# First modulation tile in four loads, bias columns in their rows, x ahead of 256 weight columns, and more warming products, at the opening of a decoder layer

## The chip, the cores and the metric

The kernel runs on one core of one Trainium2 chip. The metric is the device time of one execution in microseconds: the median of 3 runs is 735.68 us (735.65 to 735.8). The engines are named as the profile has them: TensorE (PE, with its weight loads as PEld), VectorE (DVE), ScalarE (ACT), GpSimd (POOL) and SyncE (SP), which here only issues DMAs.

## The reference

One decoder layer: attention of two kinds on a modulated input, merged by gates, and a gated feed-forward part. The change concerns only the beginning, the modulation and the first projection:

```
mod = c @ w_ada + b_ada
sh1, sc1, gt1, sh2, sc2, gt2 = [m[:, None, :] for m in jnp.split(mod, N_MOD, axis=-1)]

u = x * (1.0 + sc1) + sh1
proj = u @ w_in
q_a, k_a, v_a, f_a, q_b, k_b, v_b, g_a, g_b = jnp.split(proj, _split_points(), axis=-1)
```

x has 512 rows of 1024 columns, w_ada is 1024 by 6144, w_in 1024 by 5128. All is in 32-bit floating point. Each of the six parts of mod has 1024 values, which the kernel holds as 8 tiles of 128.

## The kernel before

**Products in three.** Full precision is had by splitting each operand into a high part in a reduced format (ScalarE copies it: wh of a weight, uh of the modulated input) and the rest (VectorE subtracts: wl, ul). Each product is then three: high with high, low weight with high input, high weight with low input.

**Opening.** The first stage runs over 8 tiles of 128 input channels. For tile j it needs two modulation values for each channel (kind 0, the shift, and kind 1, the scale), each a sum over 1024 products of c with a row of w_ada. VectorE forms such a sum in one instruction over a row of w_ada and a copy of c that stands in every partition (`mod_sum`, L241), and adds the bias (`bcols`). Then ScalarE or VectorE forms uh and ul of the tile (`first_mod`), ScalarE and VectorE split the 904 weight columns of the tile (`first_split`, `first_pad`), and TensorE accumulates 23 products of 512 columns (`first_mm`, L361) into the banks `grp[0..7]`: three for each of the column groups 0 to 6, and two for the padded forget gate columns (`fpad`, group 7).

**Tile 0** has its own path, since nothing can run before it. c is broadcast by 8 small products (L235) into the banks 6 and 7, and the sums for tile 0 read c from there; ScalarE copies it into `cbc` afterwards (L337), which the sums of all other tiles read. The two modulation rows of tile 0 come in two loads: `wa[0]` holds the first half of both kinds, `wa[1]` the second half of both. So there are four sums of 512 columns, two for each load. Between the third and the fourth, VectorE adds the first halves to the biases (L287); the last addition (L289) gives `modc`. The weight columns of tile 0 come as 384 and 520 columns, with x between them (L258 to L260).

**Order of the work.** Each engine runs its instructions in the order written, partly rearranged by a scheduler, which places an instruction where its model of the time finds it ready; `tc.issue_after` ties an instruction behind another on this engine. SyncE issues loads in the order written. At most eight loads are outstanding: each later one waits until the eighth before it has landed. The loads of c (4 KB) and of the biases (`bcols`, 24 KB, 192 bytes for each partition) are issued by ScalarE (L103, L105).

**Warming.** While TensorE waits for tile 0 it multiplies zeros (`heat`, L230): 5 products before the broadcast, 3 after it, and then 1, 1 and 2 behind the second, third and fourth sum.

The order of the products of tile 0 is by `rank`: high with high of the groups 0 to 2, low weight of the same, then high with high of 3 and 4, and so on.

After the first stage (from 50 us) the second one begins with the weights of the attention heads; `split_proc` (L217 on ScalarE, L94 on VectorE) splits them.

Of the kernel before, what the change touches and what calls it, by code (L numbers as in the profile page):

```python
# [46 lines left out]
CUT = 5  # L47
FILL = (15, 18, 18), (11, 11, 11)
# [3 lines left out]
def layer_kernel(ctx: ExitStack, tc: tile.TileContext, out, xT, x, c8, wa0, wa1, bcol, w1, wct, wv, bf,  # L52
# [50 lines left out]
    S.dma_start(c8s, c8)  # L103
    bcols = const([P, 6, KT], F32, "bcols")
    bcd = S.dma_start(bcols, bcol)  # L105
# [24 lines left out]
    for q in (slice(1, 2), slice(3, 6)):  # L130
        S.activation(bcols[:, q, :], bcols[:, q, :], AF.Copy, bias=1.0)
# [97 lines left out]
    def heat(n):  # L229
        return [PE.matmul(grp[5], warm[:, 0:P], warm, start=True, stop=True) for _ in range(n)]  # L230
# [17 lines left out]

    x0 = early.tile([P, 512], F32, name="x0", tag="x0")

    def first_load(j):
        wa = [early.tile([P, D], F32, name=nm("wa"), tag="wa", bufs=5) for _ in range(2)]
        r = stg.tile([P, 1024], F32, name=nm("raw"), tag="raw", bufs=LOADS)
        xt = z(F32, "xt")
        if j == 0:
            for e in range(2):
                nc.sync.dma_start(wa[e], wa0[j, e])
            nc.sync.dma_start(r[:, 0:384], w1[j][:, 0:384])  # L258
            nc.sync.dma_start(x0, xT[j * P : (j + 1) * P, :])
            nc.sync.dma_start(r[:, 384:W1C], w1[j][:, 384:W1C])  # L260
        else:
            nc.sync.dma_start(wa[0], wa0[j, 0])
            if j == 1:
                nc.sync.dma_start(wa[1], wa0[j, 1])
            nc.sync.dma_start(r[:, 0:W1C], w1[j])
            if j > 1:
                nc.sync.dma_start(wa[1], wa0[j, 1])
            nc.sync.dma_start(xt, xT[j * P : (j + 1) * P, :])
            if j == 6:
                nc.sync.dma_start(bfs, bf)  # L270
        pend[j] = [wa, xt, r]

    def first_acc(j):
        wa = pend[j][0]
        if j == 0:
            s = state["chl"]
            for e in range(2):
                for q in range(2):
                    c = slice(q * 512, (q + 1) * 512)
                    with tc.issue_after(s.ins):  # L280
                        s = mod_sum(q, j, wa[e], c, e, grp[6 + e])
                    if e or q:
                        for m in heat(WARM[2] + e * q):
                            paced(m, s)
                    if e and not q:
                        with tc.issue_after(s.ins):
                            s = V.tensor_tensor(bcols[:, 0:2, j], bcols[:, 0:2, j], modr[:, 0:2, j, 0], ALU.add)  # L287
# [6 lines left out]
    def first_split(j):  # L294
# [3 lines left out]
        if j:  # L298
            hi_of(h[:, 0:W1C], r[:, 0:W1C])
        else:  # L300
            state["h"] = S.activation(h[:, 0:384], r[:, 0:384], AF.Copy)
        pend[j][2:] = [h, l, r]

    def first_pad(j):
        h, l, r = pend[j][2:]
        if j == 0:
            c = slice(384, W1C)
# [5 lines left out]
    def first_mod(j):  # L313
# [12 lines left out]
        else:  # L326
# [5 lines left out]
            c = slice(384, W1C)  # L332
# [5 lines left out]
            with tc.issue_after(ts.ins):  # L338
                ts = lo_of(l[:, 0:384], r[:, 0:384], h[:, 0:384])
# [15 lines left out]
    def first_mm(j, gs):  # L355
        ops = [(g, n, m) for g in gs for n, m in enumerate(first_ops(j, g))]
        if j < KT - 1:
            rank = (0, 2, 4, 1, 3, 5)
            ops.sort(key=(lambda o: rank[o[1]] + 3 * (o[0] > 2) if o[0] < 5 else o[1] + 3 * (o[0] == 7)) if j == 0 else lambda o: o[1] + 3 * (o[0] == 7))
# [976 lines left out]
def _pack(inputs):  # L1336
# [10 lines left out]
    wa0 = wt[0:2].transpose(1, 0, 2, 3).copy()  # L1347
    wa0[0] = wa0[0].reshape(2, P, 2, D // 2).transpose(2, 1, 0, 3).reshape(2, P, D)
    r["wa0"] = c(wa0)
    r["wa1"] = c(wt[2:6].reshape(32, P, D))  # L1350
    bm = a["b_ada"].reshape(6, KT, P)
    r["bcol"] = c(bm[[0, 1, 3, 4, 2, 5]].transpose(2, 0, 1))
# [29 lines left out]
_NAMES = ["xT", "x", "c8", "wa0", "wa1", "bcol", "w1", "wct", "wv", "bf", "wp", "wo", "lncol", "lnrow",  # L1382
# [20 lines left out]
```

## Time and profile before

| what | value |
|---|---|
| median of 3 runs | 735.68 us |
| the profiled execution, whole | 736.08 us |
| its span, first to last instruction | 734.3 us |
| mean granted TensorE clock | 0.997 |
| TensorE busy | 724.3 us, 99% |
| VectorE busy | 599.7 us, 82% |
| ScalarE busy | 390.1 us, 53% |
| first product of the layer | 8.00 us |
| TensorE busy from 8.00 to 50.40 us | 42.40 of 42.40 us |
| TensorE busy from 470 to 727 us | 256.49 of 257.00 us |
| TensorE busy from 727 us to the end | 0.00 of 7.30 us |

TensorE works almost without a pause from the first product of the layer to 727 us; before it lies the opening, behind it the last normalisation. How such a profile is read: a row of the timeline gives the start, the length, the engine, the line, what is written and read, and in brackets the idle time of this engine just before with what ended it. PE rows that stand for several products give the length of all of them together.

### The profile page before, as it was taken

Reading aid. Unit: us, or ns where it says so; the run is one execution under the profiler, and the core shown is the slowest. Engines: PE = TensorE matmul, PEld = TensorE weight load, DVE = VectorE, ACT = ScalarE, POOL = GpSimd, SP = SyncE. Lnnn points to the kernel's source line nnn. Section 1 sums busy time; section 2 is a strip of 40 time slices with the busy share of each in tenths; the row PEclk is TensorE's granted clock in tenths of the full one; section 3 lists DMA queues with packets and bytes.
Section 4 is the critical chain, followed back from the end, with each engine's and each line's share of the span. In section 5 each row is a group of like instructions: output and inputs, shape, how many; then the busy total and the mean of one; then the engine's idle time right before and its main releaser. Section 6 shows DMA issues by size and latency. Waiting matters only on the chain.

```text
span 734.3 us, 9843 instructions
## 1 busy us (share of the span) xinstructions
PE 724.3 (99%) x3442; PEld 604.8 (82%) x3442; DVE 599.7 (82%) x1049; ACT 390.1 (53%) x681; POOL 84.5 (12%) x140
## 2 busy tenths in 40 slices
PE   8999999999999999999999999999999999999995
PEld 5888888888888888888889888888888888888885
DVE  7878799778899896883697999977887878679996
ACT  5576466596885755432065644444453544346550
POOL 1026224343010000000000001000011001000010
PEclk9999999999999999999999999999999999999998
DMA  9944534523332242632075687577799767656734
GB/s 351 404 167 147 196 116 160 185 65 119 135 117 79 95 153 77 206 145 86 1 258 134 218 249 230 177 242 229 206 345 248 212 224 212 214 168 219 228 83 92
DMA packets 45203, 131.96 MB, mean 180 GB/s; under 512 B 6137, under 2 KB 6657, under 8 KB 45153
## 3 DMA queue, kind: packets, MB, share of 16 engines
q1 hardware_dynamic: 37888, 112.61, 44.3%
q0 software_dynamic: 4224, 10.30, 7.4%
q10 hardware_dynamic: 3040, 8.42, 3.1%
q8 instruction: 27, 0.44, 0.2%
q14 instruction: 24, 0.19, 0.1%
HBM read 118.39 MB, written 12.85 MB: 179 GB/s over the span
## 4 chain that ended last, share of the span: by engine, by line
PE 98%; DVE 1%; DMA 0%; issue 0%; DVEq 0%
PE ps L152 19%; PE ps L154 19%; PE ps L153 19%; PE ps L361 6%; PE ps L1131 5%; PE ps L1133 5%; PE ps L1132 5%; PE ps L599 3%; PE ps L581 2%; PE ps L507 2%; PE ps L509 2%; PE ps L508 2%; PE ps L924 2%; PE ps L922 2%; PE ps L923 2%; PE ps L533 1%
## 5 line engine op out<-in xcount | busy, mean ns | idle before, releaser
L217 ACT ACTIVATE wh<-raw 128x1024 fp32r<-128x1024 f32 (+1 forms) x105 | 109.2, 1042 | 107.4 <-PE ps L153 35.2
L94 DVE TENSOR_TENSOR wl<-raw,wh 128x1024 fp32r<-128x1024 f32 (+2 forms) x114 | 137.8, 1210 | 34.2 <-ACT wh L217 33.5
L152 PE MATMUL ps<-u2h,wh 128*128 128x512 f32 (+1 forms) x376 | 141.3, 376 | 0.0
L153 PE MATMUL ps<-u2l,wh 128*128 128x512 f32 (+1 forms) x376 | 141.2, 375 | 0.0
L154 PE MATMUL ps<-u2h,wl 128*128 128x512 f32 (+1 forms) x376 | 141.2, 375 | 0.0
L154 PEld LDWEIGHTS ps<-u2h,wl 128*128 128x128 f32 x376 | 70.8, 188 | 12.9
L152 PEld LDWEIGHTS ps<-u2h,wh 128*128 128x128 f32 x376 | 70.8, 188 | 12.7
L153 PEld LDWEIGHTS ps<-u2l,wh 128*128 128x128 f32 x376 | 70.8, 188 | 12.7
L152 PE MATMUL ps<-uh,wh 128*128 128x512 f32 x200 | 79.5, 398 | 0.0
L154 PE MATMUL ps<-uh,wl 128*128 128x512 f32 x200 | 78.3, 391 | 0.0
L153 PE MATMUL ps<-ul,wh 128*128 128x512 f32 x200 | 77.9, 390 | 0.0
L1184 ACT ACTIVATE cv<-ps,cw 128x512 f32<-128x512 f32 x44 | 34.0, 773 | 46.2 <-PE ps L154 36.2
L1185 DVE SCALAR_TENSOR_TENSOR cv<-ps,cw,cv 128x511 f32<-128x511 f32 x44 | 32.8, 745 | 22.6 <-ACT cv L1184 22.5
L154 PEld LDWEIGHTS ps<-uh,wl 128*128 128x128 f32 x200 | 37.5, 188 | 8.6 <-DVE wl L94 0.3
L153 PEld LDWEIGHTS ps<-ul,wh 128*128 128x128 f32 x200 | 37.6, 188 | 7.5
L152 PEld LDWEIGHTS ps<-uh,wh 128*128 128x128 f32 x200 | 37.5, 188 | 7.3
L241 DVE SCALAR_TENSOR_TENSOR raw<-raw,cbc 128x1024 f32<-128x1024 f32 x32 | 39.6, 1238 | 0.0
L561 POOL TENSOR_TENSOR pt<-pt,om 128x127 f32<-128x127 f32 (+3 forms) x32 | 38.5, 1213 | 1.6 <-DVE om L560 1.5
L181 POOL DMA_DIRECT2D raw<-in_wdp x10 | 8.8, 884 | 245.1 <-DMA raw<-in_wdp 208.4
L1186 DVE SCALAR_TENSOR_TENSOR cv<-ps,cw,cv 128x510 f32<-128x510 f32 x44 | 32.7, 743 | 0.4
L1192 ACT ACTIVATE cv<-cv 128x512 f32<-128x512 f32 x22 | 13.9, 631 | 34.1 <-DVE cv L1186 34.1
L560 DVE TENSOR_TENSOR_SCAN om<-om,dg 128x127 f32<-128x127 f32 (+3 forms) x32 | 27.1, 907 | 2.9 <-ACT om L555 2.9
(238 smaller groups left out, 1552.5 us busy)
## 6 DMA issues: line engine op xcount, KB each, us to landing
raw<-in_wup SPq DMA_DIRECT2D x44, 512.0 KB, 4.7
raw<-in_wa SPq DMA_DIRECT2D x32, 512.0 KB, 3.5
raw<-in_wct SPq DMA_DIRECT2D x25, 512.0 KB, 4.5
raw<-in_wdp SPq DMA_DIRECT2D x20, 512.0 KB, 5.6
wa<-in_wa SPq DMA_DIRECT2D x16, 512.0 KB, 8.6
raw<-in_wdp SPq DMA_DIRECT2D x22, 256.0 KB, 4.5
raw<-t SPq DMA_DIRECT2D x22, 256.0 KB, 4.1
raw<-in_wdp POOLq DMA_DIRECT2D x10, 512.0 KB, 7.4
```

The costliest lines, as they stand in the source:

```text
L94: state["read"] = V.tensor_tensor(o, i, fl(hi), ALU.subtract)
L152: PE.matmul(ps, wh, ah, start=first, stop=False)
L153: PE.matmul(ps, wh, al, start=False, stop=False)
L154: return PE.matmul(ps, wl, ah, start=False, stop=last)
L217: state["hi"] = S.activation(h[:, 0:cols], r[:, 0:cols], AF.Copy)
L241: state["read"] = V.scalar_tensor_tensor(wt[:, c], wt[:, c], 1.0, cbc[:, c] if by is None else by, ALU.mult, ALU.mult, accum_out=o)
L361: PE.matmul(grp[g], w, u, start=j == 0 and n == 0, stop=j == KT - 1 and n == (1 if g == 7 else 2))
L561: G.tensor_tensor(pt[b][:, s : e - 1], pt[b][:, s : e - 1], om[:, s + 1 : e], ALU.mult)
L1131: PE.matmul(ps, ah, bh, start=first, stop=False, skip_group_check=onto)
L1132: PE.matmul(ps, ah, bl, start=False, stop=False, skip_group_check=onto)
L1133: return PE.matmul(ps, al, bh, start=False, stop=last, skip_group_check=onto)
L1184: S.activation(t, ps, AF.Identity, bias=cw[:, n, 3:4], scale=cw[:, n, 2:3])
```

## The change

- The two loads of tile 0's modulation rows become four, in the order in which the sums use them: first half of kind 0, first half of kind 1, second half of kind 0, second half of kind 1. The first two go to `wa[0]`, the others to a new tile `wz`.
- The biases no longer have a load of their own. They are stored behind the last quarter, so that each row of the fourth load has 560 values rather than 512. ScalarE copies them from `wz` into `bcols`, in four instructions, adding 1 where that is needed; before, it added the 1 in place, in two.
- x is loaded before the weight columns of tile 0, and these come as 256 and 648 columns, not 384 and 520. The first products of tile 0 are those of the groups 0 and 1.
- Behind the second, third and fourth sum, one more warming product of 256 columns each.

```diff
-    S.dma_start(c8s, c8)
+    bcd = S.dma_start(c8s, c8)
     bcols = const([P, 6, KT], F32, "bcols")
-    bcd = S.dma_start(bcols, bcol)
...
-    for q in (slice(1, 2), slice(3, 6)):
-        S.activation(bcols[:, q, :], bcols[:, q, :], AF.Copy, bias=1.0)
...
+    wz = early.tile([P, D + 6 * KT], F32, name="wz", tag="wz")
     x0 = early.tile([P, 512], F32, name="x0", tag="x0")
...
         if j == 0:
-            for e in range(2):
-                nc.sync.dma_start(wa[e], wa0[j, e])
-            nc.sync.dma_start(r[:, 0:384], w1[j][:, 0:384])
+            wa.append(wz)
+            for k in range(4):
+                c, w = k % 2 * 512, 512 if k < 3 else 512 + 6 * KT
+                nc.sync.dma_start(wa[k // 2][:, c : c + w], wz0[:, k * 512 : k * 512 + w])
             nc.sync.dma_start(x0, xT[j * P : (j + 1) * P, :])
-            nc.sync.dma_start(r[:, 384:W1C], w1[j][:, 384:W1C])
+            nc.sync.dma_start(r[:, 0:W0], w1[j][:, 0:W0])
+            nc.sync.dma_start(r[:, W0:W1C], w1[j][:, W0:W1C])
...
-                        for m in heat(WARM[2] + e * q):
+                        for m in heat(WARM[2] + e * q, 1):
                             paced(m, s)
...
-            state["h"] = S.activation(h[:, 0:384], r[:, 0:384], AF.Copy)
+            bz = wz[:, D:].rearrange("p (a b) -> p a b", b=KT)
+            for q, b in ((0, 0.0), (1, 1.0), (2, 0.0), (slice(3, 6), 1.0)):
+                S.activation(bcols[:, q, :], bz[:, q, :], AF.Copy, bias=b)
+            state["h"] = S.activation(h[:, 0:W0], r[:, 0:W0], AF.Copy)
...
-            rank = (0, 2, 4, 1, 3, 5)
-            ops.sort(key=(lambda o: rank[o[1]] + 3 * (o[0] > 2) if o[0] < 5 else o[1] + 3 * (o[0] == 7)) if j == 0 else lambda o: o[1] + 3 * (o[0] == 7))
+            ops.sort(key=(lambda o: o[1] + 3 * (o[0] > 1) if o[0] < 5 else o[1] + 3 * (o[0] == 7)) if j == 0 else lambda o: o[1] + 3 * (o[0] == 7))
```

The rest of the diff is the 256 (`W0`) in place of 384 in the later steps of tile 0 and the new layout of the input arrays.

Two places show what becomes of the order. First ScalarE at the opening (in front of each arrow stands what is written, behind it what is read), before the change:

```order
L103 DMA c8s<-in_c 8x128
L105 DMA bcols<-in_bcol 128x48
L116 ACT_TABLE_LOAD
L116 ACTIVATE sgt<-ones 128x1
L131 ACTIVATE bcols<-bcols 128x8
L131 ACTIVATE bcols<-bcols 128x24
L301 ACTIVATE wh_187<-raw_172 128x384
L331 ACTIVATE xt_173<-x_169,modc 128x512
L334 ACTIVATE wh_187<-raw_172 128x520
```

and with it:

```order
L104 DMA c8s<-in_c 8x128
L116 ACT_TABLE_LOAD
L116 ACTIVATE sgt<-ones 128x1
L304 ACTIVATE bcols<-wz 128x8 x3
L304 ACTIVATE bcols<-wz 128x24
L305 ACTIVATE wh_186<-raw_169 128x256
L335 ACTIVATE xt_170<-x_167,modc 128x512
L338 ACTIVATE wh_186<-raw_169 128x648
```

The load of the biases is gone, and four copies that read the fourth load (`wz`) stand where two additions stood.

VectorE's order there is unchanged; the addition of the first halves reads `bcols` between the third and the fourth sum, as before. SyncE's first loads before the change:

```order
L257 DMA wa_170<-in_wa 128x1024
L257 DMA wa_171<-in_wa 128x1024
L258 DMA raw_172<-in_w 128x384
L259 DMA x_169<-in_xT 128x512
L260 DMA raw_172<-in_w 128x520
L262 DMA wa_179<-in_wa 128x1024
```

and with it:

```order
L258 DMA wa_168<-in_wz 128x512 x2
L258 DMA wz<-in_wz 128x512
L258 DMA wz<-in_wz 128x560
L259 DMA x_167<-in_xT 128x512
L260 DMA raw_169<-in_w 128x256
L261 DMA raw_169<-in_w 128x648
L263 DMA wa_178<-in_wa 128x1024
```

Two loads more stand ahead of tile 1's first one, and x has moved ahead of the first weight columns.

The last place is ScalarE at tile 7, the last of the first stage, which the edit doesn't name: uh and xt belong to tile 7, and the `wh` of 1024 columns are the first two weights of the second stage. Before:

```order
L217 ACTIVATE wh_604<-raw_596 128x1024
L318 ACTIVATE uh_511<-xt_446,modc 128x512
L323 ACTIVATE xt_446<-xt_446,modc 128x512
L91 ACTIVATE fpad<-raw_445 128x8
L217 ACTIVATE wh_608<-raw_598 128x1024
L645 ACTIVATE sg_577<-ps_145 128x512
```

and with the change:

```order
L215 ACTIVATE wh_610<-raw_602 128x1024
L322 ACTIVATE uh_517<-xt_452,modc 128x512
L215 ACTIVATE wh_614<-raw_604 128x1024
L327 ACTIVATE xt_452<-xt_452,modc 128x512
L92 ACTIVATE fpad<-raw_451 128x8
L648 ACTIVATE sg_583<-ps_142 128x512
```

The second of these weight splits now stands ahead of xt, which ul is made from. On TensorE, tile 7's first product that reads ul was the sixth and is now the eleventh.

More of the change, by code (lines that the diff above doesn't have):

```diff
@@ L47, with layer_kernel @@
 CUT = 5
+W0 = 256
 FILL = (15, 18, 18), (11, 11, 11)
 @with_exitstack
-def layer_kernel(ctx: ExitStack, tc: tile.TileContext, out, xT, x, c8, wa0, wa1, bcol, w1, wct, wv, bf,
+def layer_kernel(ctx: ExitStack, tc: tile.TileContext, out, xT, x, c8, wa0, wa1, wz0, w1, wct, wv, bf,
                  wp, wo, lncol, lnrow, wup, cwb, wdp):
@@ L228, in layer_kernel, with heat @@
         G.memset(fl(fpad), 0.0)
-    def heat(n):
-        return [PE.matmul(grp[5], warm[:, 0:P], warm, start=True, stop=True) for _ in range(n)]
+    def heat(n, more=0):
+        return [PE.matmul(grp[5][:, 0:w], warm[:, 0:P], warm[:, 0:w], start=True, stop=True) for w in [512] * n + [256] * more]
     heat(WARM[0])
@@ L247, in mod_col @@
         return V.tensor_tensor(o, modr[:, w, col, 0:1], b, ALU.add)
+    wz = early.tile([P, D + 6 * KT], F32, name="wz", tag="wz")
     x0 = early.tile([P, 512], F32, name="x0", tag="x0")
     def first_load(j):
-        wa = [early.tile([P, D], F32, name=nm("wa"), tag="wa", bufs=5) for _ in range(2)]
+        wa = [early.tile([P, D], F32, name=nm("wa"), tag="wa", bufs=5) for _ in range(2 if j else 1)]
         r = stg.tile([P, 1024], F32, name=nm("raw"), tag="raw", bufs=LOADS)
@@ L306, in first_pad @@
         if j == 0:
-            c = slice(384, W1C)
+            c = slice(W0, W1C)
             lo_of(l[:, c], r[:, c], h[:, c])
@@ L331, in first_mod @@
                 u = S.activation(xt, x0, AF.Identity, bias=sh, scale=sc)
-            c = slice(384, W1C)
+            c = slice(W0, W1C)
             with tc.issue_after(u.ins):
@@ L338, in first_mod @@
             with tc.issue_after(ts.ins):
-                ts = lo_of(l[:, 0:384], r[:, 0:384], h[:, 0:384])
+                ts = lo_of(l[:, 0:W0], r[:, 0:W0], h[:, 0:W0])
             with tc.issue_after(ts.ins):
@@ L1346, in _pack @@
     wt = c(w_ada.T).reshape(6, KT, P, D)
-    wa0 = wt[0:2].transpose(1, 0, 2, 3).copy()
-    wa0[0] = wa0[0].reshape(2, P, 2, D // 2).transpose(2, 1, 0, 3).reshape(2, P, D)
-    r["wa0"] = c(wa0)
+    r["wa0"] = c(wt[0:2].transpose(1, 0, 2, 3))
     r["wa1"] = c(wt[2:6].reshape(32, P, D))
     bm = a["b_ada"].reshape(6, KT, P)
-    r["bcol"] = c(bm[[0, 1, 3, 4, 2, 5]].transpose(2, 0, 1))
+    bcol = bm[[0, 1, 3, 4, 2, 5]].transpose(2, 0, 1).reshape(P, 6 * KT)
+    halves = [wt[q, 0][:, e * 512 : (e + 1) * 512] for e in range(2) for q in range(2)]
+    r["wz0"] = c(np.concatenate(halves + [bcol], axis=1))
     def col(kind, n):
@@ L1379, in _pack @@
     return r
-_NAMES = ["xT", "x", "c8", "wa0", "wa1", "bcol", "w1", "wct", "wv", "bf", "wp", "wo", "lncol", "lnrow",
+_NAMES = ["xT", "x", "c8", "wa0", "wa1", "wz0", "w1", "wct", "wv", "bf", "wp", "wo", "lncol", "lnrow",
           "wup", "cwb", "wdp"]
```

## Prediction

> **What bounds the kernel now.** I read the summary of the chain of waits first:
>
> ```profile
> span 734.3 us, 9843 instructions
> PE 98%; DVE 1%; DMA 0%; issue 0%; DVEq 0%
> ```
>
> TensorE (PE) ends nearly everything, so an edit counts only if it moves the start of that run of products or puts a gap into it. The same chain in order of time (start, length, what) shows the start:
>
> ```profile
> 0.74 3.45 DMA wa<-in_wa
> 4.30 1.30 DVE wa L241 x4
> 5.65 0.17 DVE wa L241
> 5.82 0.44 issue
> 6.42 0.62 DVE wa L241 x2
> 7.06 0.16 DVE modc L289
> 7.31 0.56 DVE uh L329
> 7.87 0.14 issue
> 8.00 42.38 PE ps L361 x184
> ```
>
> The first modulation load lands at 4.19 us, VectorE forms four sums, modc is done at 7.22, and the first product of the layer starts at 8.00. Then 184 products run back to back, 0.23 us each. Two rows of the list of waits concern them:
>
> ```profile
> PE ps L361 <- DVE uh L329: 0.3, 1, 0.3
> PEld ps L361 <- ACT uh L318: 0.2, 1, 0.2
> ```
>
> The first is the start at 8.00. The second, on the weight loads alone, is tile 1: its uh is ready just as PE finishes tile 0's 23 products (8.00 + 23 x 0.23 = 13.3). Tile 1 has next to no slack, so **an earlier tile 0 is worth only what tile 1 gains too**. What holds tile 1, from the timeline:
>
> ```profile
> 9.64 1.22 DVE L241 SCALAR_TENSOR_TENSOR wa<-wa,cbc 128x1024 f32<-128x1024 f32 x1
> 11.94 0.28 DVE L247 TENSOR_TENSOR modc<-modr,bcols 128x1 f32<-128x1 f32 x2
> 11.57 0.96 ACT L91 ACTIVATE wh<-raw 128x904 fp32r<-128x904 f32 x1 [1.87 <-DMA raw<-in_w]
> 12.44 0.80 ACT L318 ACTIVATE uh<-xt,modc 128x512 fp32r<-128x512 f32 x1
> ```
>
> Its modc is ready at 12.22, but uh starts at 12.44: ScalarE stands in wh, which waited 1.87 us for the eighth load of SyncE's stream. So tile 1 hangs on the DMA stream, with modc 0.2 us behind as the next bound.
>
> **The change, part by part.** The sum starts from the profiled execution: span 734.3, 736.08 us in all, 0.40 above the median of 735.68; the difference found is put on the median.
>
> *Four loads instead of two.* The stretches of DMA traffic around the opening (length; busy time of PE, PEld, DVE, ACT, POOL; PEclk, DMA share, GB/s):
>
> ```profile
> 3.50:4.00 0.50, 0.50 (x8) 0.50 (x6) 0.00 (x0) 0.00 (x0) 0.50 (x3) 1.00 1.01 401
> 4.50:5.00 0.50, 0.50 (x2) 0.15 (x1) 0.50 (x3) 0.00 (x0) 0.50 (x2) 1.00 0.91 308
> 5.00:5.50 0.50, 0.50 (x2) 0.00 (x0) 0.50 (x1) 0.00 (x0) 0.39 (x1) 1.00 1.23 305
> 5.50:6.00 0.50, 0.50 (x2) 0.10 (x1) 0.45 (x3) 0.23 (x2) 0.00 (x0) 1.00 0.76 244
> 6.00:6.50 0.50, 0.22 (x2) 0.10 (x1) 0.50 (x4) 0.09 (x1) 0.00 (x0) 1.00 1.04 391
> ```
>
> At 401 GB/s, 256 KB take 0.65 us. My estimate of the landings: first quarter 4.19 - 0.65 = 3.54, second 4.19, third 4.84, fourth (280 KB) 5.54; I take 5.6. At the dip's mean of 286 GB/s the last two would take 1.9 us: 6.1, the upper bound. Two more issues on SyncE cost nothing: at 0.43 us each (the x row below) SyncE stays ahead of 0.65 us of data.
>
> *The sums.* Rows of ScalarE and VectorE (start, length), and of TensorE:
>
> ```profile
> 5.65 0.69 DVE L241 SCALAR_TENSOR_TENSOR wa<-wa,ps 128x512 f32<-128x512 f32 x1
> 6.26 0.16 DVE L287 TENSOR_TENSOR bcols<-bcols,modr 128x2 f32<-128x2 f32 x1
> 6.34 0.68 DVE L241 SCALAR_TENSOR_TENSOR wa<-wa,ps 128x512 f32<-128x512 f32 x1
> 5.77 0.32 ACT L131 ACTIVATE bcols<-bcols 128x8 f32<-128x8 f32 x2 [2.50 <-DMA bcols<-in_bcol]
> 3.37 1.04 PE L235 MATMUL ps<-crow,sel 128*128 128x128 bf16 x8
> ```
>
> One sum takes 0.61 us of VectorE (5.65 to 6.26), the small addition 0.08, the last sum to modc 0.72 (6.34 to 7.06), modc 0.16. With the quarter at 3.54, the first sum waits instead for the broadcast of c: four of the eight products fill its bank, so between 3.9 (half of 1.04) and 4.41 (all); I take 4.05. Three sums end at 4.05 + 3 x 0.61 = 5.88, against 6.26.
>
> *Bias columns in the fourth load.* Here **a new wait stands in the chain**: the addition needs the biases of the first two kinds, which ScalarE now copies out of the fourth load. Two such copies took 0.32 us, so the addition starts at 5.6 + 0.04 + 0.32 + 0.03 = 5.99, not 5.88. VectorE runs in order, so the last sum stands behind it. Then modc ends at 5.99 + 0.08 + 0.72 + 0.16 = 6.95, against 7.22: **0.27 us gained**; 0.38 if the load lands by 5.5, a loss of 0.2 if at 6.1. The other two copies (0.23 more) end before ScalarE's next input.
>
> *x ahead of 256 columns.* The issue and the landing of x:
>
> ```profile
> 2.13 0.43 SPq L259 DMA_DIRECT2D x<-in_xT  x1
> x<-in_xT SPq DMA_DIRECT2D x1, 256.0 KB, 5.1
> ```
>
> x landed at 7.23, as late as modc; without this move the gain would end there. Now it lands at 5.6 + 0.65 = 6.25 and the 256 columns at 6.6, both before 6.95. With 2 x 3 products before the other columns' rather than 3 x 3, TensorE reaches the third group four products after its start. Relative to the end of modc: TensorE starts at +0.78, is there at +1.75, and ScalarE has split the other 648 columns at +1.55 (xt from +0.08, then 0.62 + 0.1 for 128 more columns). ul and the rest of wl are also ready first. No gap. But that larger split lies ahead of the cbc copies:
>
> ```profile
> 8.02 0.62 ACT L334 ACTIVATE wh<-raw 128x520 fp32r<-128x520 f32 x1
> 8.55 1.06 ACT L337 ACTIVATE cbc<-ps 128x512 f32<-128x512 f32 x2
> ```
>
> so tile 1's sums start 0.1 us later after modc: of 0.27, 0.17 reaches its modc, which had 0.2 to spare; 0.37 is open there.
>
> *The stream up to tile 1's weights* carries the same bytes. What differs is the separate load of 24 KB in 192-byte rows, in whose time the rate dips: 92, 95 and 156 GB/s short for 0.5 us each is 0.43 us lost at 401. If that load is the cause, the stream gains 0.43 less 0.06 for its bytes, 0.37; if not, 0, less up to 0.1 for more and smaller loads. I take the middle, 0.2, because only the coincidence ties them. A sentence of its own for the page: the Trainium skill, "DMA: Bandwidth & Descriptors", Specifications, gives 512 bytes as the least transfer for full rate, below which the engine reads, modifies and writes; by it the dip is the columns' and the stream's term 0.37, while by my halving it is 0.2.
>
> *TensorE.* Tile 0 gains 0.27, tile 1 0.2, and later tiles follow, since the list of waits has no further row for them. The warming products stand in waiting time; the last three, from 6.9, end by 7.5 at the full pitch, before the start at 7.73.
>
> *A move that the diff does not show* is at tile 7: the scheduler now puts the second stage's weight split ahead of the ScalarE step xt, and the products with ul later. Before:
>
> ```profile
> 43.21 0.81 ACT L323 ACTIVATE xt<-xt,modc 128x512 f32<-128x512 f32 x1
> 44.67 1.06 ACT L217 ACTIVATE wh<-raw 128x1024 fp32r<-128x1024 f32 x1 [0.55 <-PE ps L361]
> 44.06 0.69 DVE L94 TENSOR_TENSOR ul<-xt,uh 128x512 fp32r<-128x512 f32 x1 [0.71 <-ACT xt L323]
> 44.93 0.39 PE L361 MATMUL ps<-uh,wh 128*128 128x512 f32 x1
> ```
>
> That split waits for tile 6's last product, so xt now starts at 44.67 + 0.97 = 45.64 on this clock (1.06 less the 0.09 by which steps of ScalarE overlap, as 11.57 and 12.44 show), ul runs 0.85 behind it as now, to 47.18, and TensorE can take it 0.13 later (7.87 to 8.00), at 47.31. Ten other products stand first: 44.93 + 10 x 0.23 = 47.23. A gap of 0.08; between 0 and 0.25. ScalarE's next steps slide by some 1.2 us. Who waits for them:
>
> ```profile
> 50.68 1.41 DVE L94 TENSOR_TENSOR m<-ps,m 64x512 fp32r<-64x512 f32 x2 [1.05 <-ACT m L91]
> ```
>
> The first of these two ends at 51.4, and its reader on TensorE stands in the chain at
>
> ```profile
> 53.16 0.11 PE ps L533
> ```
>
> so 0.5 us of the 1.7 are left. If that cover went too, each 0.1 later would cost 0.1.
>
> The sum: -0.2 + 0.08 = -0.12 us, with -0.2 if the gap closes. Forecast **735.5** (735.68 less 0.15).
>
> **Rivals.**
>
> *Gain of 0.3 to 0.45.* The 192-byte rows were the whole dip: stream 0.37, modc 0.38. For it: the dip coincides. Against: tile 1's modc leaves no more than 0.37. 735.3.
>
> *Nothing.* The dip has another cause, tile 1's weights land when they did, PE waits at tile 1 for what tile 0 gained. 735.7.
>
> *The new wait costs more than the old (slower).* Place: the addition before the last sum. It decides at a fourth load landing at 6.26 - 0.39 = 5.87 us; each 0.1 later costs 0.1. At 6.1 and with the gap at tile 7 of 0.2: 736.1. For it: the load's rows are the longest, at the end of four. Against: the stream without the dip reaches it at 5.54.
>
> *The clock lapses (slower).* Warming products:
>
> ```profile
> 1.20 2.31 PE L230 MATMUL ps<-warm 128*128 128x512 bf16 x5 [1.20 <-DVE warm L107]
> 4.20 1.93 PE L230 MATMUL ps<-warm 128*128 128x512 bf16 x4
> 7.08 0.60 PE L230 MATMUL ps<-warm 128*128 128x512 bf16 x2 [0.29 <-DVE wa L241]
> ```
>
> Five at 0.42 us apart, four still so until about 5.7, the last two at 0.21: half rate for 4.5 us, then full rate, although PEclk says 1.00. If the rearranged waits let it fall back, tile 0 starts at half rate for as long: 4.5 us for 11 products instead of 20, 9 x 0.23 = 2.1 lost, 737.7. Against: the pauses between warming products (0.3 us) get shorter, if anything. The Trainium skill ("TensorE: Matmul & The Clock Gate", Part 1) says that a free-running window of about 3.4 us of activity opens or closes the gate; by it the loss is 1.6 and the time 737.2, and pauses of 0.3 us don't close it, which the rows above bear out.
>
> **How the numbers follow.** Forecast 0.5, larger gain 0.14, nothing 0.19, new wait slower 0.14, clock 0.03. The range, 735.1 to 736.1, takes in the first four with the bounds of the landings. A measurement can tell about 0.2%, 1.5 us: only the clock rival passes that above (0.03), nothing worked out passes it below (0.01).
>
> **What would show it.** The fourth load's landing and the addition's start (5.99); modc's end (6.95); the first product (7.73); ScalarE's wait for tile 1's weights, now ending near 11.35; no dip at 4.5 to 6 us; a PE gap near 47. A gap at tile 1 would make the forecast wrong, as would products 0.43 apart.

## The result and the profile after

The kernel with the change takes **738.01 us** in the median of 10 runs (736.84 to 739.48), the kernel before beside it 735.90 (735.65 to 737.49). The ratio is 1.0027, with a 95% interval of 1.0018 to 1.0035: slower by 0.27%. The forecast of 735.5 and its range (735.1 to 736.1) miss it. The profiled execution took 737.38 us, with a span of 735.6 (734.3 before).

The rows that answer to the opening of before, from the timeline of the changed kernel (start, length, engine, line, what is written and read, idle time ahead and what ended it):

```profile
3.97 0.69 DVE L239 SCALAR_TENSOR_TENSOR wa<-wa,ps 128x512 f32<-128x512 f32 x1 [0.81 <-PE ps L233]
4.58 0.68 DVE L239 SCALAR_TENSOR_TENSOR wa<-wa,ps 128x512 f32<-128x512 f32 x1
5.75 0.69 DVE L239 SCALAR_TENSOR_TENSOR wz<-wz,ps 128x512 f32<-128x512 f32 x1 [0.47 <-DMA wz<-in_wz]
6.84 0.16 DVE L288 TENSOR_TENSOR bcols<-bcols,modr 128x2 f32<-128x2 f32 x1 [0.40 <-ACT bcols L304]
7.64 0.16 DVE L290 TENSOR_TENSOR modc<-modr,bcols 128x2 f32<-128x2 f32 x1
6.50 0.52 ACT L304 ACTIVATE bcols<-wz 128x8 f32<-128x8 f32 x4 [3.64 <-DMA wz<-in_wz]
12.34 0.96 ACT L92 ACTIVATE wh<-raw 128x904 fp32r<-128x904 f32 x1 [1.97 <-DMA raw<-in_w]
```

The first two sums run as early as forecast (3.97, 4.58). Then VectorE waits for the third quarter until 5.75, and ScalarE for the fourth until 6.50. The addition starts at 6.84, modc ends at 7.80 (7.22 before), and tile 0's first product starts at 8.53 (8.00 before). What sets the start of tile 1, though, is the DMA stream, as the chain of waits shows (start, length, what):

```profile
4.97 7.35 DMA raw<-in_w
12.34 0.69 ACT wh L92
13.20 0.81 ACT uh L322
14.06 0.96 PE ps L364 x3
```

Tile 1's weights are there at 12.34 (11.57 before), its modc at 12.88, and ScalarE starts uh only at 13.20, when the split of the weights lets it. TensorE has a gap there: tile 0's last product starts at 13.61, the next at 14.06, where 0.23 us is the pace. The DMA traffic in the same stretches as before (last two columns: busy share of the DMA engines, GB/s):

```profile
3.50:4.00 0.50, 0.50 (x8) 0.50 (x6) 0.03 (x1) 0.00 (x0) 0.50 (x2) 1.00 0.94 238
4.50:5.00 0.50, 0.50 (x3) 0.10 (x1) 0.50 (x3) 0.00 (x0) 0.50 (x1) 1.00 0.79 275
5.00:5.50 0.50, 0.33 (x2) 0.11 (x2) 0.28 (x2) 0.00 (x0) 0.25 (x1) 1.00 0.90 304
```

Between 3.5 and 4 us it moves 238 GB/s, where the kernel before moved 401. At tile 7, the list of waits of TensorE's weight loads (waited for: total, times, longest) and the timeline show:

```profile
PEld ps L535 <- DVE fq L410: 0.3, 1, 0.3
PEld ps L364 <- DVE ul L95: 0.2, 1, 0.2
45.41 1.06 ACT L215 ACTIVATE wh<-raw 128x1024 fp32r<-128x1024 f32 x1 [1.45 <-PE ps L364]
46.38 0.80 ACT L327 ACTIVATE xt<-xt,modc 128x512 f32<-128x512 f32 x1
54.10 0.74 DVE L410 SCALAR_TENSOR_TENSOR fq<-ps,bfs,fq 8x512 f32<-8x512 f32 x1
54.47 0.28 PE L536 MATMUL ps<-m,s 128*128 128x256 f32 x1
54.89 0.51 PE L535 MATMUL ps<-m,s 128*128 128x512 f32 x1
```

The second split waits for TensorE, xt stands behind it, and all that ScalarE does next is late, down to fq (the copy of the forget gate out of its PSUM bank) on VectorE. The fourth score product writes into that bank, so it starts at 54.89 instead of about 54.6.

**How far TensorE is behind.** The same product stands in both traces at two times. The table gives these times less those of the kernel with the old loads (c_oldloads, below), in us, at tile 1, at the start of tile 7's products (46 us), behind the score products of the second stage (56 us), and at the last product:

```
                tile 1   46 us   56 us   last
before again      0.01    0.01    0.01   0.17
after             0.83    0.83    1.31   1.90
a_order           2.71    2.71    2.71   3.03   (clock fell)
b_contig          0.79    0.79    0.79   1.03
b_again           1.30    1.30    1.30   1.79
b_slide           0.52    0.52    0.97   1.47
p_rows            0.35    0.35    0.35   0.36
e_biasfirst       0.42    0.44    0.44   0.54
w_one             1.38    1.39    1.39   1.94
w_one_slide       1.30    1.30    1.30   1.64
n_nowarm          2.60    2.60    2.60   2.58
```

The labels are those of the runs told of below. What the opening loses is never given back; only tile 7 adds to it in `after` and `b_slide`. What comes later (0 to 0.6) was not traced to a cause; the kernel before shows as much (0.50 in its first profile).

**Two kinds of execution.** Each run lists its mean granted clock. Five of the ten runs of the changed kernel have 0.996 to 0.998 and took 736.84 to 737.64; the other five have 0.994 or 0.995 and took 738.38 to 739.48.

### The profile page after: what moved, and what is told of

Read it like the earlier page. It is cut to its first block, busy times and chain, and to the rows that moved or that the text cites. A ratio compares the mean times of both kernels' runs of the same rounds, so it can differ in the third digit from the quotient of the medians.

```text
span 735.6 us, 9852 instructions
## 1 busy us (share of the span) xinstructions
PE 724.7 (99%) x3445; PEld 604.9 (82%) x3445; DVE 600.9 (82%) x1049; ACT 390.3 (53%) x683; POOL 85.2 (12%) x140
## 4 chain that ended last, share of the span: by engine, by line
PE 96%; DMA 1%; DVE 1%; ACT 1%; SPq 1%; issue 0%; DVEq 0%
PE ps L150 19%; PE ps L152 19%; PE ps L151 19%; PE ps L1134 5%; PE ps L1136 5%; PE ps L1135 5%; PE ps L364 5%; PE ps L602 3%; PE ps L584 2%; PE ps L510 2%; PE ps L512 2%; PE ps L511 2%; PE ps L927 2%; PE ps L925 2%; PE ps L926 2%; PE ps L535 1%
## 5 line engine op out<-in xcount | busy, mean ns | idle before, releaser
L150 PEld LDWEIGHTS ps<-u2h,wh 128*128 128x128 f32 x376 | 70.8, 188 | 13.2 <-issue 0.5
```

The source lines that it names most:

```text
L150: PE.matmul(ps, wh, ah, start=first, stop=False)
```

## The experiments

Three causes were to be told apart: the loads land late; TensorE's clock falls back in the longer pauses of the warming; the order at tile 7 costs. Times are medians, "before" is the kernel before measured beside it, and a lapse is a run with a mean granted clock of 0.995 or less. (A stretch of 3.41 us at half rate takes 0.0023 off the mean; a stretch at half rate behind the last product, 2.6 to 5.5 us in the traces, takes off 0.0017 to 0.0037 in any run. So a single run at 0.995 or 0.996 can be put down wrongly.) Of each edit the main lines are shown.

| run | median us | before | ratio, 95% interval | lapses |
|---|---|---|---|---|
| before_again | 735.94 | 736.02 | 0.9998 [0.9989, 1.0007] | 0 of 11 |
| a_order | 737.70 | 736.02 | 1.0021 [1.0010, 1.0031] | 5 of 9 |
| c_oldloads | 735.78 | 736.02 | 0.9998 [0.9989, 1.0007] | 0 of 11 |
| e_biasfirst | 736.56 | 736.02 | 1.0008 [0.9999, 1.0017] | 1 of 11 |
| b_contig | 736.57 | 736.01 | 1.0008 [0.9999, 1.0017] | 1 of 10 |
| w_warm | 737.95 | 736.01 | 1.0025 [1.0016, 1.0034] | 0 of 11 |
| m_merge | 737.30 | 736.01 | 1.0019 [1.0010, 1.0029] | 3 of 10 |
| w_one | 736.88 | 735.94 | 1.0010 [1.0001, 1.0018] | 0 of 10 |
| w_one_slide | 736.76 | 735.94 | 1.0011 [1.0003, 1.0020] | 1 of 11 |
| n_nowarm | 737.92 | 735.94 | 1.0023 [1.0010, 1.0035] | see below |
| q_two | 739.02 | 735.94 | 1.0039 [1.0026, 1.0051] | 5 of 6 |
| p_rows | 736.28 | 735.91 | 1.0007 [0.9998, 1.0016] | 1 of 10 |
| p_four | 739.70 | 735.91 | 1.0048 [1.0034, 1.0061] | see below |
| b_slide | 737.54 | 735.91 | 1.0023 [1.0014, 1.0032] | 4 of 11 |
| b_again | 736.61 | 735.91 | 1.0013 [1.0003, 1.0024] | 4 of 11 |

s_split ran once, 737.15. One run of w_one with an odd clock record (0.947, 737.4) isn't counted among its lapses. The kernel before itself has 5 lapses in the 110 runs beside these.

### Which part of the change it is

before_again:

> The kernel before, unchanged, for the spread of its time and of its granted clock. Theory A (the changed kernel loses 0.74 us to a later DMA stream at the opening, 0.5 us to the slid ScalarE steps at tile 7, and what its median lies above its profiled run to a lower TensorE clock in some executions): the ratio is 1.000, the clock 0.997 in nearly all executions, spread under 1 us. Rival B (the two kernels differ by nothing but the state of the chip): clock and time scatter here as widely as with the change, over 2 us.

a_order ties the second split of stage 2 behind tile 7's x, as it was before:

```diff
-            with tc.issue_after(state["k" if state["proc"] else "after"].ins):
+            with tc.issue_after(state["k" if state["proc"] else "after"].ins), tc.issue_after(state["u" if state["proc"] else "after"].ins):
```

> The changed kernel with the second weight split of the second stage tied behind xt of tile 7 on ScalarE, as in the kernel before; all else as changed. Theory A: the gap of 0.3 us before the fourth score product and the one of 0.08 at ul go, the profiled span falls by 0.5 to about 735.1, and the median by as much against the changed kernel's 738.0. Rival (the slid steps are hidden, the 0.5 us are a second effect of the opening): no difference, span 735.6.

c_oldloads, on top of it, takes back the loads and the biases (x ahead of 256 columns, the order of the products and the warming stay):

```diff
-            for k in range(4):
-                c, w = k % 2 * 512, 512 if k < 3 else 512 + 6 * KT
-                nc.sync.dma_start(wa[k // 2][:, c : c + w], wz0[:, k * 512 : k * 512 + w])
+            for e in range(2):
+                nc.sync.dma_start(wa[e], wa0[j, e])
```

> As a_order, but with the two loads of the modulation and the separate load of the biases as in the kernel before; x ahead of 256 weight columns, the order of tile 0's products and the added warming products stay. Theory A (the quarter loads slow the stream): the last modulation load lands near 5.6 us again, modc ends near 7.2, x is there at 6.5, the first product starts at 7.9 to 8.0, tile 1 at 13.3; ratio 0.9995 to 1.0005. Rival (x and the short weight loads slow the stream): tile 1 stays near 14.0 and the ratio near 1.001 or above.

e_biasfirst keeps the two loads but stores the biases in the rows of the first, so that the load of 192-byte rows is gone:

```diff
-                nc.sync.dma_start(wa[e], wa0[j, e])
+            nc.sync.dma_start(wz, wz0)
+            nc.sync.dma_start(wa[1], wa0[j, 1])
```

> As c_oldloads, but the biases stand in the rows of the first of the two modulation loads (4288 bytes a row), so neither the 192-byte load nor a wait for the last load is left. Theory A with the dip of the kernel before put down to the 192-byte load: no dip at 4.5 to 6 us, the second load lands at 5.3, modc ends near 6.9, tile 1 starts near 13.0, ratio 0.9993 to 0.9998. Rival (the dip comes with the first short loads, whatever they carry): the second load still lands near 5.6, tile 1 near 13.3, ratio 1.000.

before_again agrees with before, so the comparison holds. In a_order the shift of tile 7 is gone (2.71 before it and behind it in the table), but the median gains only 0.3 us on the changed kernel, as five of nine runs lapse; the four without have a median of 736.72, against 737.38 for the five such runs of the changed kernel. c_oldloads is as fast as the kernel before: **the rest of the change is worth nothing that shows (0.9998, 0.9989 to 1.0007), and the loss hangs on the four loads with the biases and on the order at tile 7**. In e_biasfirst the dip stays, as its stretches of traffic show:

```profile
4.50:5.00 0.50, 0.50 (x5) 0.22 (x4) 0.50 (x1) 0.43 (x4) 0.50 (x4) 1.00 0.72 275
5.00:5.50 0.50, 0.50 (x3) 0.14 (x1) 0.50 (x3) 0.00 (x0) 0.50 (x1) 1.00 0.82 274
```

So the load in 192-byte rows was not its cause. By the Trainium skill ("DMA: Bandwidth & Descriptors", Specifications) a transfer needs at least 512 bytes for full rate, and those rows have fewer; the dip of 275 and 274 GB/s without them speaks against that as its cause here.

The profiled execution of a_order caught a lapse. Its TensorE in three stretches (length; busy time of PE first; PEclk, the granted clock, is the third column from the end) and two rows of the timeline:

```profile
6.19:9.61 3.42, 1.82 (x8) 0.81 (x8) 2.25 (x9) 1.86 (x7) 0.00 (x0) 1.00 0.96 344
9.61:13.02 3.41, 3.41 (x9) 2.63 (x8) 3.35 (x6) 1.62 (x5) 0.00 (x0) 0.50 1.03 414
13.02:16.40 3.38, 3.38 (x16) 2.77 (x15) 2.65 (x8) 2.87 (x5) 0.00 (x0) 1.00 1.02 411
8.22 0.71 PE L228 MATMUL ps<-warm 128*128 128x512 bf16 x3 [1.22 <-DVE wz L239]
9.63 1.05 PE L364 MATMUL ps<-uh,wl 128*128 128x512 f32 x2
```

From 6.19 to 9.61 TensorE is busy for 1.82 of 3.42 us; for exactly the next 3.41 us the granted clock is 0.50 and it runs 9 products, where the stretch behind takes 16. Seven products of 0.23 us are missing, 1.6 us. Two other profiles caught the same: m_merge behind a stretch with 1.68 us of work, q_two behind 1.49. A stretch with 1.87 kept the clock in b_again, one with 1.91 in `after`, one with 2.19 in before_again. The edge is thus near 1.8 to 1.9 us, not sharp: w_one kept it with 1.80, in the execution with the odd clock record.

### Why the loads land late

b_contig: a_order with each of the first three quarters in a block of its own in memory (`wq0`) instead of every 8384 bytes:

```diff
-                nc.sync.dma_start(wa[k // 2][:, c : c + w], wz0[:, k * 512 : k * 512 + w])
+                nc.sync.dma_start(wa[k // 2][:, c : c + w], (wq0[k] if k < 3 else wz0))
```

> As a_order, but the first three quarters of tile 0's modulation weights lie each in a block of its own in the chip's memory (rows of 2048 bytes one behind the other) instead of every 8384 bytes; the same four loads, the same sizes of packets. If each load in the opening has a price of about 0.9 to 1.0 us of its own, whatever its bytes, nothing changes: third quarter seen by VectorE at 5.6 to 5.9 us, fourth at 6.4 to 7.1, first product of tile 0 at 8.5 to 9.1, 737.7 us in the median like a_order. If the distance between the rows is what slowed them, the third is seen at 4.9 and the fourth at 5.6, the first product at 7.8 to 8.0, and the time is that of the kernel before, 735.5 to 736.0.

s_split: c_oldloads with the last 648 weight columns in four loads.

```diff
-            nc.sync.dma_start(r[:, W0:W1C], w1[j][:, W0:W1C])
+            for k in range(4):
+                c = slice(W0 + 162 * k, W0 + 162 * (k + 1))
+                nc.sync.dma_start(r[:, c], w1[j][:, c])
```

> As c_oldloads (two loads of 512 KB and a bias load), but tile 0's last 648 weight columns come in four loads of 162 columns instead of one: the same bytes, three loads more ahead of tile 1's. If a load costs 0.9 to 1.0 us of the queue however small it is, the weights of tile 1 land 2.1 to 2.9 us later than in c_oldloads and the first product of tile 1 starts at 15.4 to 16.2 us instead of 13.32; the time is 738 or more, as tile 0 has no work to fill the hole. If bytes set the time, or the slow landing belongs to the very first microseconds alone, tile 1 starts by 13.8 at the latest and the time is 735.8 to 736.3.

m_merge: c_oldloads with x and all weight columns of tile 0 in one load.

```diff
-            nc.sync.dma_start(x0, xT[j * P : (j + 1) * P, :])
-            nc.sync.dma_start(r[:, 0:W0], w1[j][:, 0:W0])
-            nc.sync.dma_start(r[:, W0:W1C], w1[j][:, W0:W1C])
+            nc.sync.dma_start(xw, xw0)
```

> As c_oldloads, but x and all 904 weight columns of tile 0 come in one load with rows of 5664 bytes behind the two modulation loads: three loads of tile 0 on SyncE's queue instead of five. If each load under about 400 KB costs 0.9 to 1.0 us whatever its size, the merged load (725 KB, 1.8 us at 401 GB/s) takes the place of three that take 2.7 us: all of it by 6.6 to 7.0 us, tile 1's weights 0.5 to 0.8 us earlier than in c_oldloads, tile 1's first product at 12.8 to 13.3 instead of 13.32, and the time 735.2 to 735.8. If bytes set the time, the three loads and the one end together, and the time is 735.6 to 736.0; if the merged load lands later than x alone did, past the modulation's end at 7.1, the first product is late and the time is 736 or more.

A row of each kernel's timeline, in this order: the third sum in b_contig, the split of tile 1's weights in s_split, the step that needs x in m_merge.

```profile
5.82 0.69 DVE L239 SCALAR_TENSOR_TENSOR wz<-wz,ps 128x512 f32<-128x512 f32 x1 [0.54 <-DMA wz<-in_wq]
```

```profile
12.75 0.96 ACT L92 ACTIVATE wh<-raw 128x904 fp32r<-128x904 f32 x1 [2.94 <-DMA raw<-in_w]
```

```profile
8.71 0.55 DVE L329 TENSOR_SCALAR uh<-xw,modc 128x512 fp32r<-128x512 f32 x1 [1.36 <-DMA xw<-in_xw]
```

In b_contig the third quarter is seen at 5.82, as in `after`: the distance of the rows is not what makes it late. Its time, though, is nearer to before than a_order's, mostly because the clock lapsed once instead of five times: the expectation had taken a_order's median for the price of the loads. In s_split three more loads delay tile 1 by 1.15 us, 0.38 each: neither the 0.9 of a fixed price nor next to nothing, as by bytes. Part of it can be the limit of eight loads outstanding: with three more ahead, SyncE issues tile 1's first load at 5.80 us, in c_oldloads at 3.10. **The theory of a fixed price of 0.9 us a load fell.** m_merge fell too: x is seen at 8.71, not by 7.0. The traffic ran at 373 and 380 GB/s meanwhile (7.5 to 8.5 us), but it was shared with the loads behind, and everything now waits for the end of the whole 708 KB.

Two runs were to separate the size of the pieces from the number of loads. p_rows moves the two loads of c_oldloads in pieces of 2048 bytes, as the quarters are; p_four splits each of them into two of 64 rows, with pieces of 4096 bytes:

```diff
+                nc.sync.dma_start(wa[e].rearrange("p (q c) -> p q c", q=2), wq0[2 * e : 2 * e + 2].rearrange("q p c -> p q c"))
...
+                for h in (slice(0, 64), slice(64, P)):
+                    nc.sync.dma_start(wa[e][h], wa0[j, e][h])
```

> As c_oldloads, with its two loads of 512 KB, but each made of pieces of 2048 bytes instead of 4096 (each half row lies in a block of its own in memory): the size of the pieces of the quarters, and the number of loads of the kernel before. If small pieces are what slowed the quarters, the second load is seen at 6.0 us or later instead of 5.3 to 5.7, the first product of tile 0 starts at 8.4 or later, tile 1 at 13.7 or later, and the time is 736.3 to 736.9. If the number of loads did it, nothing changes: first product 8.0, tile 1 at 13.3, 735.5 to 736.1.

> As c_oldloads, but each of the two loads of 512 KB is issued as two of 256 KB, of 64 rows of 4096 bytes each: the number of loads of the change, with the pieces of the kernel before. If the number of loads slowed the quarters, the second half of the weights is seen at 6.0 us or later, the first product starts at 8.4 or later, tile 1 at 13.7 or later, 736.3 to 736.9. If the pieces of 2048 bytes did it, nothing changes: first product 8.0, tile 1 at 13.3, 735.5 to 736.1.

The traffic in p_rows, and then in p_four:

```profile
3.50:4.00 0.50, 0.50 (x8) 0.50 (x6) 0.00 (x0) 0.00 (x0) 0.50 (x4) 1.00 1.07 410
4.50:5.00 0.50, 0.50 (x3) 0.10 (x1) 0.50 (x3) 0.00 (x0) 0.39 (x1) 1.00 1.11 405
```

```profile
3.50:4.00 0.50, 0.50 (x8) 0.50 (x6) 0.00 (x0) 0.00 (x0) 0.50 (x5) 1.00 0.77 151
4.50:5.00 0.50, 0.50 (x2) 0.15 (x1) 0.00 (x0) 0.30 (x2) 0.44 (x1) 1.00 0.88 172
```

With small pieces in two loads the traffic holds 405 to 410 GB/s, so the pieces alone don't lower it. p_four, at 151 to 172, can't be held for or against the number of loads: by the packet records its pieces of 4096 bytes take 0.29 us each (median), where those of c_oldloads take 0.16, while the pieces of 2048 bytes take 0.084 in `after` as in p_rows. Half the rows in a load thus makes the pieces themselves slower, which the change doesn't do. (Part of p_four's 4 us is the clock, at half rate until 13.7.)

What settles it is one stretch, 3.5 to 5.5 us, in all profiles but those of p_four and q_two (below); here in `after`, and then in p_rows:

```profile
3.50:5.50 2.00, 1.83 (x13) 1.02 (x11) 1.30 (x4) 0.00 (x0) 1.75 (x5) 1.00 0.88 266
```

```profile
3.50:5.50 2.00, 1.59 (x12) 0.91 (x9) 1.23 (x4) 0.00 (x0) 1.39 (x4) 1.00 1.09 394
```

The eight profiles with the modulation rows in two loads have 341 to 394 GB/s there, the eight with four loads of 128 rows 224 to 317. **The number of loads (and with it their size) lowers the traffic, not the size of the pieces**, nor the biases in the rows (e_biasfirst, with two loads, has 341); the distance of the rows adds at most a smaller part (224 to 278 with rows every 8384 bytes, 283 to 317 with rows one behind the other). Tile 1's weights are there at 11.44 to 11.92 with two loads (s_split and m_merge, whose other loads differ, left out) and at 12.03 to 12.88 with four.

In time the runs separate this less well. Without lapses the medians lie over before by 0.35 in p_rows, 0.40 in e_biasfirst, 0.4 in b_contig and b_again, and 0.7 in a_order (4 runs). So p_rows met neither of its two expectations: its first product (8.11) and its traffic are those of the old loads, its time and tile 1's weights (11.87 instead of 11.52) lie between. What two loads with other rows lose there stays open.

How a load ends is in the packet records too. The fourth quarter alone has pieces of 2240 bytes, and the first weight columns, two loads behind it, pieces of 1024, so their packets can be told apart (first start to last end, us):

```
           fourth quarter   first weight columns   ScalarE goes on with the quarter
after      4.14 to 6.12     5.86 to 7.11           6.50
a_order    4.06 to 6.68     6.06 to 7.87           7.06
b_slide    4.32 to 5.65     5.75 to 6.83           6.00
w_one      4.09 to 6.95     5.44 to 7.94           7.33
```

In `after`, a_order and w_one the columns begin while the quarter, two loads ahead, still moves: if each DMA engine takes the loads in order, they drift apart by more than the load between, and the quarter is there when the last one is done with it. ScalarE goes on 0.35 to 0.38 us after that. And the quarter's first pieces are the slow ones: the first 16 in `after` take 0.198 us on average, the other 112 have a median of 0.091. This fits a price that each load pays at its start, but it was not tried, and why a load's start is slow was not shown.

q_two tried two queues: ScalarE issues the second and the fourth quarter on its own queue.

```diff
+    S.dma_start(wy[:, 512:D], wz0[:, 512:D])
+    bcd = S.dma_start(wz[:, 512 : D + 6 * KT], wz0[:, D + 512 : 2 * D + 6 * KT])
```

> As a_order, but the second and the fourth quarter of tile 0's modulation weights (the fourth with the biases) are issued by ScalarE on its own queue instead of SyncE's; the same four loads. [...] If the engines themselves are slow in these microseconds, whatever the queue, the fourth is seen at 6.4 or later, the first product at 8.5 or later, and the time is 736.4 to 737.6 as in a_order.

VectorE's third sum no longer waits (5.64), but the fourth quarter comes later than in any other run, as ScalarE's wait in this kernel shows:

```profile
7.68 0.52 ACT L306 ACTIVATE bcols<-wz 128x8 f32<-128x8 f32 x4 [3.95 <-DMA wz<-in_wz]
```

On a queue of its own it shares the engines with x and the weights, which stood behind it before: its packets run from 4.79 to 7.21, those of the first weight columns from 5.09. Two queues give up the order of use, and five of six runs lapse. On the price of a load within one queue it decides nothing.

### The clock

w_warm puts seven more warming products behind the second sum and five behind the third; w_one one behind each; w_one_slide is w_one without a_order's tie; n_nowarm is the kernel before without the four products behind the sums.

```diff
-                        for m in heat(WARM[2] + e * q, 1):
+                        for m in heat(WARM[2] + e * q + (0 if e and q else 5 if e else 7), 1):
...
+                        for m in heat(WARM[2] + 1, 1):
```

> As a_order, but with seven more warming products of 512 columns behind the second sum and five more behind the third, so that TensorE has no pause over 0.4 us between 4.2 us and the first product; nothing else is moved. If a lapse of TensorE's clock in the pauses (0.7 to 1.2 us) is what makes about half the runs of a_order 1.5 to 2 us longer, then the runs lie within 1 us of one another, at granted clocks of 0.996 and up, with a median of 736.5 to 736.9; products of tile 0 follow one another at 0.22 us. If the spread has another cause, the median stays at 737.5 to 738 with the spread of a_order, 736.5 to 739.4.

> As a_order, but one more warming product of 512 columns behind the second sum and one more behind the third (each of the last three sums is followed by two of 512 and one of 256), since w_warm's fourteen more ran at half rate and held TensorE back. If TensorE's clock falls back when the busy time in a stretch of 3.41 us is under about 1.85 us (1.82 and 1.69 fell, 1.91 did not), then 0.2 to 0.4 us more in the pauses keeps it: granted clock of 0.996 and up in nine runs of ten or more, median 736.5 to 736.9, first product of tile 0 still at 8.5 to 9.0. If the fall has another cause, about half the runs show 0.995 or less again and the median is 737.3 to 737.9.

> As w_one, but with the change's own order at tile 7: the second split of stage 2 comes ahead of tile 7's x on ScalarE, as in the changed kernel. If the slide of ScalarE's forget-gate copy holds the fourth score product back, this is 0.4 to 0.7 us slower than w_one at the same clock, 737.0 to 737.6. If that slide is covered, as the prediction took it, the two agree within 0.15 us.

> The kernel before, without the five warming products that it puts behind the sums of tile 0 (one behind the second, one behind the third, two behind the fourth of 512 columns, as far as these are there); loads, order and sums are as before. TensorE is then idle from about 5.6 us to its first product at 8.0 us. If pauses in the opening lower TensorE's clock, by the busy time in stretches of 3.41 us, nearly every run loses a stretch: products of tile 0 0.43 us apart, granted clock of 0.995 or less, 737.0 to 738.0. If the clock is not at work in the opening, nothing waits for these products, and the time stays at 735.7 to 736.2.

w_warm has no lapse, as expected, but its own warming holds the products back:

```profile
4.16 6.04 PE L228 MATMUL ps<-warm 128*128 128x512 bf16 x22
9.95 0.70 PE L364 MATMUL ps<-uh,wh 128*128 128x512 f32 x2
```

Its warming products are 0.43 us apart until 7.1 us and 0.22 behind that, so 22 of them end at 9.9, more than a microsecond after uh and the weights are ready (uh starts at 7.67, and runs 0.55). The expectation reckoned with full rate. Full rate begins at another time in each execution: 4.1 us in b_again, 4.5 in `after`, 5.9 in c_oldloads, 7.1 in w_warm, 7.5 in s_split, spread over 3.5 us, about the length of the stretch. Whether a pause falls into one stretch or two is chance, and so is a lapse.

w_one has the dose right: **no lapse in 10 runs, one in 11 with w_one_slide; with the change's own warming it is 19 in 51** (`after` 5 of 10, a_order 5 of 9, b_contig 1 of 10, b_again 4 of 11, b_slide 4 of 11; the first two, 10 of 19, have the strided loads of w_one and w_one_slide). Its fourth quarter landed late in the profiled execution (7.33), with the first product at 9.37, and still no product ran at half rate. n_nowarm shows the reverse with the old loads: TensorE pauses from 5.6 to 7.98 us, its products are 0.43 us apart until 13.2, and it is 2 us slower. (Full rate comes first at 13.5 us there, and at 13.7 in p_four; the mean clock does not count the time ahead of it, so such a run shows no lapse.)

### The order at tile 7

w_one_slide was to price it but didn't: with one more warming product the scheduler put the instructions of tile 7 in the order of before. b_slide and b_again (b_contig once more) have the change's warming and differ in that order alone:

```diff
-            with tc.issue_after(state["k" if state["proc"] else "after"].ins), tc.issue_after(state["u" if state["proc"] else "after"].ins):
+            with tc.issue_after(state["k" if state["proc"] else "after"].ins):
```

> As b_contig, but with the instruction order that the changed kernel has at tile 7: on ScalarE the second split of stage 2 stands ahead of tile 7's x, and TensorE takes the four products that need no x remainder for two more banks ahead. Nothing else differs from b_contig. If the slide of the forget-gate copy costs what the shift of the changed kernel shows (0.83 us behind before at tile 7's start, 1.31 at the end of the score products), this is 0.3 to 0.7 us slower than b_again beside it. If that shift came from elsewhere, the two agree within 0.2 us.

> b_contig once more, in the same call as b_slide, so that the two are compared on one chip: 736.3 to 736.9 by its first runs, with a lapse of the clock (granted clock of 0.995 or less) in one or two runs of ten, against five of ten for the changed kernel's strided quarters if the lapses go with how late the fourth quarter lands.

Without the lapses, 4 of 11 in both, the medians are 737.01 (7 runs) and 736.30 (7): **0.7 us**, the upper end of what was expected (the two groups overlap: 736.81 to 737.65 and 735.60 to 737.13). The score products, of b_slide and then of b_again:

```profile
54.15 0.28 PE L536 MATMUL ps<-m,s 128*128 128x256 f32 x1
54.57 0.50 PE L535 MATMUL ps<-m,s 128*128 128x512 f32 x1
```

```profile
54.84 0.28 PE L536 MATMUL ps<-m,s 128*128 128x256 f32 x1
54.96 0.40 PE L535 MATMUL ps<-m,s 128*128 128x512 f32 x1
```

The step between them is 0.42 us with the slide and 0.12 without, and the table above has 0.45 between 46 and 56 us. The profiles thus show 0.45, the medians 0.7; the rest lies within their scatter. The list of waits names fq for 0.3 us in b_slide, as in `after`, and has no such row in b_again.

**The sum**, with terms from medians of 4 to 7 runs. Opening: b_again without lapses is 0.4 us over before (736.30 against 735.91), a_order 0.7 (736.72, 4 runs, against 736.02). Tile 7: 0.5 to 0.7. Clock: a lapse costs 1.5 us in the changed kernel (738.87 against 737.37, means of five runs each), in half the runs, so 0.75 in the middle. Together 1.65 to 2.15, and 2.1 was measured; how the opening's part divides between the loads' number, their rows and scatter stays open. No kernel here beats the one before.

## Where the prediction was right and where wrong

- **The landings: the step that failed first.** "At 401 GB/s, 256 KB take 0.65 us" did not hold behind the first two quarters, for which no sum waited: the third was seen at 5.75 (forecast 4.84), the fourth at 6.50 (5.6, with 6.1 as the upper bound). The rate was read from a stretch with loads of 512 KB, and the price of four loads was put at "less up to 0.1 for more and smaller loads" without a reason; this was the term that carried the change. The runs showed 224 to 317 GB/s with four loads where two have 341 to 394. Even the bound, taken from the dip's rate of 286 GB/s, was passed, since the change's own dip began at 3.5 us with 238.
- **The bias copies, the addition, modc.** The chain was right and only its input late: from the fourth load's arrival to the end of modc the forecast has 6.95 - 5.6 = 1.35, measured 7.80 - 6.50 = 1.30. The rival of the new wait named place and point of decision (5.87) correctly and got 0.14; its price stopped at 736.1 because the bound of the landing did.
- **x ahead of 256 columns, no gap in tile 0.** Right in `after`: there is no pause of TensorE between 8.53 us and tile 1, and c_oldloads, which keeps this part, equals before. But it gains nothing by itself either, and where the stream is later still the gap comes: in b_again ScalarE has the 648 columns only at 9.09, and the shift grows by 0.7 within tile 0.
- **The stream.** Wrong in sign, and the term that the sum rests on: tile 1's weights came 0.77 later instead of 0.2 earlier, and with ScalarE's split they set the start of tile 1, 0.83 behind the old loads. That tile 1 hangs on the stream was right, and the gap there is one of the prediction's own signs of being wrong. The halved term of 0.37 for the 192-byte rows was no gain at all (e_biasfirst).
- **Tile 7.** The gap at ul was forecast as 0.08 and is 0.1 (0.83 to 0.94 in the shift of TensorE), and the slide of ScalarE of 1.2 us is there. But the reader of m, for which "0.5 us of the 1.7 are left", was not the next to be late: fq ends at 54.84 instead of about 53.6 (52.86 before, and 0.74 for the opening), and the bank that it frees is awaited by the fourth score product. That cover was not looked up. (The cover of m was itself read a little too wide: the first score products start at 52.94 and 52.99, not at 53.16.) It cost 0.5 to 0.7 where 0.08 was put.
- **The clock.** Its mechanism was right and its price of 2.1 somewhat high: a lapse costs 1.5 to 1.6 us. The window of about 3.4 us that the Trainium skill gives ("TensorE: Matmul & The Clock Gate", Part 1) agrees with the stretch of 3.41 us here. The chance of 0.03 was too low, since that the pauses "get shorter, if anything" hung on the landings: they were 0.67 and 0.66 us in `after` and 1.22 in a_order. Half the runs lapsed.

Late loads thus moved three terms that the forecast had treated as separate: modc, the stream and the clock. The slide at tile 7 is a loss of its own.

## What to carry to other kernels

Splitting a load so that its first part comes sooner can have a price in the parts behind it: take the rate for the new loads from a place with loads of this number and size, or bound it well below, and ask what the last part delays. Where warming products cover a wait, a longer wait needs more of them, but only so many that they end in time at half rate. When an engine slides, follow every reader of what it makes, those that wait for a buffer to come free too, down to the first that is late.

## What the runs showed of the hardware

- In these traces the granted clock changes in stretches of 3.41 us that begin at any phase of the execution (full rate first at 4.06 to 7.54 us, in n_nowarm and p_four at 13.5 and 13.7). With 1.49, 1.68 and 1.82 us of TensorE's work in one, the next ran at half rate; with 1.80 (once), 1.87, 1.91 and more it kept full rate.
- In the opening, from 3.5 to 5.5 us, two loads of 512 KB move 341 to 394 GB/s, with pieces of 2048 bytes (p_rows, 394) as with 4096; four of 256 KB move 224 to 317. Loads of 64 rows are slower for another reason: their pieces of 4096 bytes take 0.29 us instead of 0.16 (p_four).
- A later load on a queue can begin before an earlier one is through: packets of the first weight columns start at 5.86 in `after`, those of the fourth quarter, two loads ahead, end at 6.12. ScalarE goes on 0.35 to 0.47 us after the quarter's last packet (0.38 in `after`, 0.47 in q_two).
- Three more loads with the same bytes, in rows of 648 instead of 2592 bytes, cost 1.15 us (s_split); the rows, the number and the limit of eight loads outstanding were not separated there.
